# A fixed engine order over the sub-layer boundaries, paired adaLN units and a regrouped convolution in a two-layer hybrid trunk

## The chip, the cores and the metric

The kernel runs on one core of a Trainium2 chip. The metric is the device time of one execution in microseconds, taken as the median of several runs. The core's engines are PE (matrix products), PEld (the weight loads of PE), DVE (vector), ACT (scalar), POOL (GpSimd) and SP, whose queue issues the transfers.

## The reference

Two layers, each FFN, token mixer, FFN, are computed for two sets of 128 tokens of 1024 channels: the context tokens and the latent tokens. Both share the weights; they differ in the conditioning vector and in the start states of the scans.

```python
def _layer(x, cond, st, l, p, alpha):
    ada = (jax.nn.silu(cond) @ p['w_ada'][l] + p['b_ada'][l]).reshape(cond.shape[0], N_MOD, 1, D_MODEL)
    sh1, sc1, g1, sh2, sc2, g2, sh3, sc3, g3 = [ada[:, j] for j in range(N_MOD)]
    f1 = _swiglu(x * (1.0 + sc1) + sh1, p['ffn1_w_gate'][l], p['ffn1_w_up'][l], p['ffn1_w_down'][l])
    x = _layer_norm(alpha * x + 0.5 * g1 * f1, p['ln_g'][l, 0], p['ln_b'][l, 0])
    y, new_st = _mixer(x * (1.0 + sc2) + sh2, st, l, p)
    x = _layer_norm(alpha * x + g2 * y, p['ln_g'][l, 1], p['ln_b'][l, 1])
    f2 = _swiglu(x * (1.0 + sc3) + sh3, p['ffn2_w_gate'][l], p['ffn2_w_up'][l], p['ffn2_w_down'][l])
    x = _layer_norm(alpha * x + 0.5 * g3 * f2, p['ln_g'][l, 2], p['ln_b'][l, 2])
    return x, new_st
```

`_swiglu` is silu(h·w_gate)·(h·w_up) times w_down with 2816 hidden channels. `_mixer` multiplies h by `w_in`, runs a gated linear attention (GLA) and an mLSTM in both directions, the latter behind a three-tap convolution with silu, and merges both through `w_br_gla`, `w_br_mlstm` and `w_out`. The final states of the context tokens are outputs too. All is float32.

## The kernel before, in words

**Units.** A weight matrix is worked off in blocks of 512 columns, and a block in units of four k-tiles of 128 rows. A unit is two loads of 512 KB (`raw`, six buffers, issued on SP's queue). Each is split in two float32r parts, `hi` by ACT (L304) and `lo` by DVE (L305), seven buffers each, since a product is made of three: xh·hi (L320), xh·lo (L321), xl·hi (L322). A unit is twelve such matmuls for each of the two streams of tokens: stream 0 (context) works on unit i while stream 1 (latent) works on unit i−2 (`LAG`), so that each weight is split once and used twice.

**Sub-layers.** The six sub-layers (FFN, mixer, FFN, twice) are six phases of one list of units. Five boundaries lie between them. At one, each stream needs its last accumulator, then `ln_half` (L378 to L382: times the gate, plus the residual, statistics), `ln_finish` (L393 and L386 on DVE, the power on POOL at L387, the normalised `y` in two halves on DVE at L399), eight transposes on PE (L349), the modulation `mf` from PSUM by DVE and ACT in turn (L353, L355), and the split in `xh` (ACT L331) and `xl` (DVE L333). Only then can PE start the next phase for that stream. The residual x = y·g + b (L420, L421) follows on DVE a few units later.

**Order.** A scheduler orders each engine's instructions by priority, in the main by program order; `ln_half` and `ln_finish` of the boundaries stand in a higher priority (`PRIO`). The main loop at the program's end loads unit i+1, consumes unit i for stream 0 and unit i−2 for stream 1, and runs the due adaLN units.

**adaLN.** The shift, scale and gate vectors of later sub-layers are computed between the units: eight groups of two vectors each, a group of eight units (`ada_unit`), a unit of two 512 KB loads into `raw` buffers and four concurrent matmuls in the four column strips of PE (L168; the trace has eight records for them, since each takes two passes).

**Mixer.** `gates` (the input and forget gates of the mLSTM, with scans along time by DVE, L565 to L585) writes `Gd` to HBM (L589, SP's queue) and reads it back as `Db`, copied over the partitions (L598, SP's queue). DVE then masks `Db` (L610). The GLA follows heads by heads: `lal` (L333), `qk`, `E`, `kL` (L657 to L707, DVE), `att` (PE), `attT` (L722 to L725, DVE), `gla_o` (L728, PE). The convolution (L802 to L805) takes its middle tap on ACT and its outer taps on DVE.

## Time and profile before

| | us |
|---|---|
| runs | 1608.05, 1613.07, 1611.59 |
| median | 1611.59 |
| the profiled execution, its own time | 1617.74 |
| span of the profiled execution | 1615.9 |
| PE busy within the span | 1576.5 (98%) |
| DVE busy | 985.8 (61%) |
| ACT busy | 757.1 (47%) |
| POOL busy | 55.6 (3%) |

The span is what the trace covers; the profiled execution's own time is 1.84 us longer. The granted TensorE clock was 0.992 over the span. Busy PE includes time at a lower granted clock, so a stretch can look busy and still be slow. A wait is booked to the instruction that stood still and to what released it.

### The profile page before, as it was taken

The numbers are of one execution on the slowest core, as the hardware profiler recorded it, in microseconds if no ns is written. First come the engines' busy times: TensorE is split into PE (matmuls) and PEld (weight loads), VectorE is DVE, ScalarE is ACT, GpSimd is POOL, SyncE is SP. The second block draws the span as 40 slices with busy tenths as digits, with TensorE's granted clock in tenths as the row PEclk, the third lists the DMA queues.
The fourth block names the chain that finished last, engine by engine and source line by source line (L and its number), as shares of the span: only waits on it lengthen the run. The fifth ranks groups of instructions, "written<-read, shape, count | busy, mean of one in ns | idle before, by whom it ended". The sixth has DMA issues, their size and how long they took to land.

```text
span 1615.9 us, 20299 instructions
## 1 busy us (share of the span) xinstructions
PE 1576.5 (98%) x7323; PEld 1190.9 (74%) x7323; DVE 985.8 (61%) x1627; ACT 757.1 (47%) x1096; POOL 55.6 (3%) x102
## 2 busy tenths in 40 slices
PE   7999999999999999999999999999999999999997
PEld 3676677777777777777778878777777777777886
DVE  3544458666776568554566555775677665765555
ACT  2443334646556434444344444454755563444441
POOL 2000001000000000000000000100000000000000
PEclk9999999999999999999999999999999999999999
DMA  9777976666766776666865657665665767646661
GB/s 329 271 265 251 312 230 220 220 221 203 253 216 213 256 265 187 195 222 215 278 186 161 181 180 254 193 197 192 187 215 165 260 209 242 214 143 183 182 235 65
DMA packets 195981, 350.19 MB, mean 217 GB/s; under 512 B 17516, under 2 KB 73596, under 8 KB 195880
## 3 DMA queue, kind: packets, MB, share of 16 engines
q1 hardware_dynamic: 195320, 348.68, 66.7%
q8 instruction: 58, 0.95, 0.2%
q0 software_dynamic: 384, 0.13, 0.1%
q14 instruction: 43, 0.35, 0.1%
q10 hardware_dynamic: 176, 0.07, 0.0%
HBM read 341.30 MB, written 7.54 MB: 216 GB/s over the span
## 4 chain that ended last, share of the span: by engine, by line
PE 81%; issue 8%; DVE 5%; DMA 2%; ACT 2%; POOL 1%; SPq 0%; DVEq 0%; POOLq 0%; ACTq 0%
PE acc L320 23%; PE acc L322 22%; PE acc L321 22%; PE adaps L168 3%; DVE lo L305 2%; DMA araw<-in_w_ada 1%; PE hT L433 1%; PE num L837 1%; ACT hi L304 1%; PE num L834 1%; PE gps L531 1%; PE zps L630 0%; DMA Db<-Gd 0%; PE rg L814 0%; PE gla_o L728 0%
## 5 line engine op out<-in xcount | busy, mean ns | idle before, releaser
L305 DVE TENSOR_TENSOR lo<-raw,hi 128x1024 fp32r<-128x1024 f32 x456 | 557.0, 1223 | 355.6 <-ACT hi L304 347.3
L304 ACT ACTIVATE hi<-raw 128x1024 fp32r<-128x1024 f32 x456 | 481.6, 1059 | 413.5 <-PE acc L322 389.3
L320 PE MATMUL acc<-hi,xh 128*128 128x512 f32 x1280 | 516.5, 405 | 7.5 <-ACT xh L331 6.3
L321 PE MATMUL acc<-lo,xh 128*128 128x512 f32 x1280 | 513.1, 401 | 4.3 <-DVE lo L305 4.3
L322 PE MATMUL acc<-hi,xl 128*128 128x512 f32 x1280 | 514.1, 402 | 0.1
L320 PEld LDWEIGHTS acc<-hi,xh 128*128 128x128 f32 x1280 | 241.9, 189 | 105.0 <-issue 27.3
L321 PEld LDWEIGHTS acc<-lo,xh 128*128 128x128 f32 x1280 | 241.9, 189 | 60.4 <-DVE lo L305 9.0
L322 PEld LDWEIGHTS acc<-hi,xl 128*128 128x128 f32 x1280 | 242.3, 189 | 57.4 <-issue 4.2
L320 PE MATMUL acc<-hi,hid 128*128 128x512 f32 x320 | 126.8, 396 | 0.0
L321 PE MATMUL acc<-lo,hid 128*128 128x512 f32 x320 | 126.7, 396 | 0.0
L322 PE MATMUL acc<-hi,hid 128*128 128x512 f32 x320 | 126.4, 395 | 0.0
L168 PE MATMUL adaps<-araw,condp 128*32 128x512 f32 x512 | 74.2, 605 | 0.7 <-DMA araw<-in_w_ada 0.7
L320 PEld LDWEIGHTS acc<-hi,hid 128*128 128x128 f32 x320 | 60.1, 188 | 18.8 <-issue 4.2
L321 PEld LDWEIGHTS acc<-lo,hid 128*128 128x128 f32 x320 | 60.1, 188 | 14.4 <-issue 0.8
L322 PEld LDWEIGHTS acc<-hi,hid 128*128 128x128 f32 x320 | 60.1, 188 | 13.7
L331 ACT ACTIVATE hid<-hT 128x512 fp32r<-128x512 f32 x40 | 23.8, 597 | 82.5 <-PE hT L433 82.5
L321 PE MATMUL acc<-lo,oh 128*128 128x512 f32 x128 | 51.3, 401 | 0.0
L320 PE MATMUL acc<-hi,oh 128*128 128x512 f32 x128 | 51.1, 399 | 0.0
L322 PE MATMUL acc<-hi,ol 128*128 128x512 f32 x128 | 50.6, 395 | 0.0
L440 ACT ACTIVATE sg<-acc 128x512 f32<-128x512 f32 x40 | 23.8, 598 | 45.7 <-PE acc L322 45.7
L333 DVE TENSOR_TENSOR hid<-hT,hid 128x512 fp32r<-128x512 f32 x40 | 27.5, 691 | 28.0 <-ACT hid L331 28.0
L387 POOL TENSOR_TENSOR rstd<-rstd,mhalf 128x1 f32<-128x1 f32 x12 | 13.1, 1094 | 814.8 <-DVE rstd L386 800.7
(246 smaller groups left out, 1481.8 us busy)
## 6 DMA issues: line engine op xcount, KB each, us to landing
araw<-in_w_ada SPq DMA_DIRECT2D x128, 512.0 KB
raw<-in_w_in SPq DMA_DIRECT2D x96, 512.0 KB
raw<-in_ffn_w_down SPq DMA_DIRECT2D x88, 512.0 KB
raw<-in_ffn_w_gate SPq DMA_DIRECT2D x80, 512.0 KB
raw<-in_ffn_w_up SPq DMA_DIRECT2D x80, 512.0 KB
raw<-in_w_in SPq DMA_DIRECT2D x96, 256.0 KB
araw<-in_w_ada SPq DMA_DIRECT2D x32, 256.0 KB
raw<-in_w_br_gla SPq DMA_DIRECT2D x16, 512.0 KB
```

What stands on the lines that cost most here:

```text
L168: T.matmul(ps[32 * q:32 * q + 32, :], lhsT=condp[:, k, :], rhs=raw[q], start=(k == 0), stop=(k == KT - 1), tile_position=(0, 32 * q))
L304: A.activation(hi, raw, AF.Copy)
L305: V.tensor_tensor(lo, raw, hi.bitcast(F32), ALU.subtract)
L320: T.matmul(acc, lhsT=xh, rhs=wh, start=(k == 0), stop=False)
L321: T.matmul(acc, lhsT=xh, rhs=wl, start=False, stop=False)
L322: T.matmul(acc, lhsT=xl, rhs=wh, start=False, stop=(k == b.nk - 1))
L331: a = A.activation(dst_h, src, AF.Copy, scale=scale)
L333: v = V.tensor_tensor(dst_l, src, dst_h.bitcast(F32), ALU.subtract)
L433: T.transpose(pt[:, t, :], h[:, 128 * t:128 * (t + 1)], ident)
L440: A.activation(sg[s], acc, AF.Silu)
L531: T.matmul(ps[0:48, :], lhsT=wgt[:, k, :], rhs=mf[s][:, k, :], start=(k == 0), stop=(k == KT - 1))
L834: T.matmul(num, lhsT=sT[:, d, :], rhs=vh, start=True, stop=(s == 0))
```

## The change

Five boundaries get a function `boundary(e)`, which writes down the order of DVE, ACT and PE by hand, from the last unit e of a phase over the first three of the next. In it the first half of stream 1's down product (`half0`) is handed to DVE late, the normalised `y` is made half by ACT and half by DVE (which needs a small operation more, `nm`), `mf` is made four tiles by DVE and four by ACT, splits of the next units stand at given places, and two adaLN units fill a place in front of stream 1's transposes. The residual of both streams is made in one go two steps later. The raised priority is gone. In the FFNs the first unit of a down block takes the odd two k-tiles, where before the last one did.

adaLN units are spread anew over the phases. In the FFNs they come two at a time, eight matmuls in a row, and are loaded two units earlier into buffers of a general pool; in the mixers they come singly. None is broken up by other matmuls. Two groups have one vector only, which adds a copy, a matmul of 512 columns (`adaf`) and an addition each.

In the convolution ACT's four operations come first and DVE's eight behind them. In the mixer `gates` is called three units later, with the work behind it where it was, and the loads of ACT's function tables move to the boundaries.

```diff
+    ada_w = {}
+    def ada_load(grp, k, own):
+        raw = ada_w[grp, k] = []
+        for i in range(2):
+            l, v = grp[i % len(grp)]
+            kk = k if len(grp) == 2 else 2 * k + i
...
-        if k == 0:
-            ada_t[grp] = ms("adaps", [512])
-        ps = ada_t[grp]
-        for q in range(4):
-            T.matmul(ps[32 * q:32 * q + 32, :], lhsT=condp[:, k, :], rhs=raw[q],
-                     start=(k == 0), stop=(k == KT - 1), tile_position=(0, 32 * q))
-        if k < KT - 1:
-            return
+    def ada_units(todo):
+        with tc.manual_schedule(engines={T.engine}):
+            for grp, k in reversed(todo):
+                raw = ada_w.pop((grp, k))
+                i = ada_n[grp] = ada_n.get(grp, 0) + 1
+                if i == 1:
+                    ada_t[grp] = ms("adaps", [512])
+                for q in reversed(range(4)):
+                    kk = k if len(grp) == 2 else 2 * k + q // 2
+                    T.matmul(ada_t[grp][32 * q:32 * q + 32, :], lhsT=condp[:, kk, :], rhs=raw[q],
+                             start=(i == 1), stop=(i == parts(grp)), tile_position=(0, 32 * q))
+        for grp in dict.fromkeys(g for g, _ in todo):
+            if ada_n[grp] == parts(grp):
+                ada_sum(grp)
...
-        V.tensor_tensor(ar, ps, bt, ALU.add)
+        if len(grp) == 1:
+            V.tensor_copy(ar, ps)
+            ps = ms("adaf", [512])
+            T.matmul(ps[0:64, :], lhsT=fold2, rhs=ar, start=True, stop=True)
+            ar = t2("adar", [512])
+            V.tensor_tensor(ar[0:64, :], ps[0:64, :], bt[0:64, :], ALU.add)
+        else:
+            V.tensor_tensor(ar, ps, bt, ALU.add)
...
-            n = min(step, b.nk - k0)
+            n = (b.nk - k0) % step or step
...
+    def consume(s, u, j0=0, j1=None, defer=False):
...
+        if k0 > 0 and b.mid is not None:
+            b.mid(s)
...
-        for j in range(n):
+        for j in range(j0, n if j1 is None else j1):
...
-        if k0 + n == b.nk:
-            b.post(s, b.acc.pop(s))
+        done = k0 + n == b.nk and j1 is None
+        def post():
+            if done:
+                b.post(s, acc)
+        if done:
+            b.acc.pop(s)
+        if defer:
+            return post
+        post()
...
+    def modulate(s, xn, l, sub, between):
 
...
+        pts = []
         for g in range(2):
-            mod_tiles(s, xn, l, sub, range(4 * g, 4 * g + 4))
-
-    def mod_tiles(s, xn, l, sub, ks):
-        pt = ms("xT", [4, 128])
-        for j, k in enumerate(ks):
-            T.transpose(pt[:, j, :], xn[:, 128 * k:128 * (k + 1)], ident)
-        for j, k in enumerate(ks):
-            gm_, bm_ = modF[:, l, sub, s, 0, k:k + 1], modF[:, l, sub, s, 1, k:k + 1]
-            if j % 2 == 0:
-                V.tensor_scalar(mf[s][:, k, :], pt[:, j, :], gm_, bm_, ALU.mult, ALU.add)
-            else:
-                A.activation(mf[s][:, k, :], pt[:, j, :], AF.Identity, scale=gm_, bias=bm_)
-        sl = slice(ks[0], ks[-1] + 1)
-        g = int(ks[0] > 0 and len(ks) == 4)
-        fin["A", s, g], fin["V", s, g] = split_fm(xh[s][:, sl, :], xl[s][:, sl, :], mf[s][:, sl, :])
-
...
+            pt = ms("xT", [4, 128])
+            pts.append(pt)
+            for j in range(4):
+                k = 4 * g + j
+                T.transpose(pt[:, j, :], xn[:, 128 * k:128 * (k + 1)], ident)
+        def gb(k):
+            return modF[:, l, sub, s, 0, k:k + 1], modF[:, l, sub, s, 1, k:k + 1]
+        for k in range(4):
+            V.tensor_scalar(mf[s][:, k, :], pts[0][:, k, :], *gb(k), ALU.mult, ALU.add)
+        for k in range(4, 8):
+            if k == 6:
+                split_fm(xh[s][:, 0:4, :], xl[s][:, 0:4, :], mf[s][:, 0:4, :])
+                between()
+            gm_, bm_ = gb(k)
+            A.activation(mf[s][:, k, :], pts[1][:, k - 4, :], AF.Identity, scale=gm_, bias=bm_)
+        split_fm(xh[s][:, 4:8, :], xl[s][:, 4:8, :], mf[s][:, 4:8, :])
...
-            for n in range(2):
-                sl = slice(512 * n, 512 * n + 512)
-                V.tensor_scalar(y[:, sl], y[:, sl], mv[:, 0:1], r, ALU.subtract, ALU.mult)
-        if idx + 1 < n_sub:
             l2, sub2 = divmod(idx + 1, 3)
-            modulate(s, y, l2, sub2)
-            later.append([3, s, y, lnbc["g"], lnbc["b"], fin["V", s, 1]])
+            def apply():
+                nm = sm("nm", 1)
+                V.scalar_tensor_tensor(nm, mv[:, 0:1], -1.0, r, ALU.mult, ALU.mult)
+                A.activation(y[:, 512:], y[:, 512:], AF.Identity, scale=r, bias=nm)
+                V.tensor_scalar(y[:, :512], y[:, :512], mv[:, 0:1], r, ALU.subtract, ALU.mult)
+            def features(between):
+                modulate(s, y, l2, sub2, between)
+                later.append([s, y, lnbc["g"], lnbc["b"]])
+            steps[s] = apply, features
...
     def residuals():
 
-        for e in later:
-            e[0] -= 1
-        while later and later[0][0] <= 0:
-            _, s, y, g, b, behind = later.pop(0)
-            with tc.issue_after(behind):
+        while later:
+            s, y, g, b = later.pop(0)
+            with tc.issue_after(fin["lo"]):
...
-                for j in range(4):
-                    ch = 2 * h + j if j < 2 else 8 + 2 * h + j - 2
+                chs = [2 * h + j if j < 2 else 8 + 2 * h + j - 2 for j in range(4)]
+                for j, ch in enumerate(chs):
                     A.activation(yh[:, j, :], pt[:, j, :], AF.Identity, scale=conv_w(l, 1, ch), bias=conv_b(l, ch))
+                for j, ch in enumerate(chs):
...
+        units[first + 3][0].mid = gates
...
+            adas(((0, 8), (1, 2)), ((1, 0), (1, 1))),
+            adas(((1, 3), (1, 4)), ((1, 5),)),
...
+    def boundary(e):
+        u, u1, u2, u3 = units[e:e + 4]
+        fill = jobs[u1[4]][:2]
+        load(u1, 0)
+        load(u2, 0)
+        for a in fill:
+            ada_load(*a, True)
+        load(u3, 0)
+        with tc.manual_schedule(engines={V.engine, A.engine, T.engine}):
+            if u1[4] % 3 > 0:
+                tables = ("natural_log_exp_and_others", "silu_and_others")[u1[4] % 3 - 1]
+                tc.keep_in_program_order(A.preload_act_table_set(tables))
+            split_half(u1, 0)
+            consume(0, u)
+            half0 = consume(1, units[e - 2], defer=True)
+            split_half(u1, 2)
+            apply, features = steps.pop(0)
+            apply()
+            consume(1, units[e - 1])
+            features(lambda: split_half(u2, 0))
+            split_half(u2, 2)
+            half0()
+            consume(1, u)
+            split_half(u3, 0)
+            consume(0, u1)
+            consume(0, u2)
+            apply, features = steps.pop(1)
+            apply()
+            split_half(u3, 2)
+            ada_units(fill)
+            consume(0, u3, 0, 2)
+            features(lambda: None)
+            consume(0, u3, 2)
+    i = s0
+    while i < n + LAG:
+        if i + 1 < n and last(i):
+            boundary(i)
+            i += 3
+            continue
+        if i + 1 < n:
+            load(units[i + 1])
+        if i < n and not last(i - 3):
             consume(0, units[i])
         if i - LAG >= s0:
             consume(1, units[i - LAG])
-        if ahead and last(i - LAG):
-            with tc.issue_after(fin["V", 0, 0]), tc.issue_after(fin["A", 0, 0]):
-                load(ahead)
-        residuals()
+        if i - s0 > 2 and last(i - 5):
+            residuals()
         if i < n:
-            for a in due[i]:
-                ada_unit(*a)
+            for a in due_load[i]:
+                ada_load(*a, units[i][4] % 3 != 1)
+            ada_units(due[i])
+        i += 1
...
```

DVE at the second boundary (mixer to FFN in the first layer), around the normalisation of stream 1; `lo` is a weight split, `mv` the statistics, `mf` the modulated features, `x` the residual (`x_132` before and `x_133` now are stream 1's). Before:

```order
L378 TENSOR_TENSOR y<-acc_5459,gbc 128x512
L382 BN_STATS bst<-y 128x6
L381 SCALAR_TENSOR_TENSOR y<-x_132,y 128x512
L305 TENSOR_TENSOR lo<-raw,hi 128x1024
L382 BN_STATS bst<-y 128x6
L305 TENSOR_TENSOR lo<-raw,hi 128x1024
L393 BN_AGGR mv<-bst 128x2
L420 TENSOR_TENSOR x_131<-y,lngbc 128x1024
L386 TENSOR_SCALAR rstd<-mv 128x1
L305 TENSOR_TENSOR lo<-raw,hi 128x1024
L399 TENSOR_SCALAR y<-y,mv,rstd 128x512 x2
L421 TENSOR_TENSOR x_131<-x_131,lnbbc 128x1024
```

and now:

```order
L427 TENSOR_TENSOR y<-acc_5409,gbc 128x512
L430 SCALAR_TENSOR_TENSOR y<-x_133,y 128x512
L431 BN_STATS bst<-y 128x6
L427 TENSOR_TENSOR y<-acc_5492,gbc 128x512
L430 SCALAR_TENSOR_TENSOR y<-x_133,y 128x512
L431 BN_STATS bst<-y 128x6
L442 BN_AGGR mv<-bst 128x2
L435 TENSOR_SCALAR rstd<-mv 128x1
L334 TENSOR_TENSOR lo<-raw,hi 128x1024
L450 SCALAR_TENSOR_TENSOR nm<-mv,rstd 128x1
L452 TENSOR_SCALAR y<-y,mv,rstd 128x512
L334 TENSOR_TENSOR lo<-raw,hi 128x1024
```

The residual has left the stretch; both halves of stream 1 now stand in one row, a `lo` stands right behind `rstd` as it did, and DVE makes one half of `y`.

DVE in the first mixer, from the gates' last result `mc`, which is what `Gd` is written from, to the first `E` of the GLA. Before:

```order
L579 TENSOR_SCALAR mc<-pp_119,m0col_122 32x128 x4
L305 TENSOR_TENSOR lo<-raw,hi 128x1024
L585 TENSOR_TENSOR mt<-cumS,GT 128x8 x2
L305 TENSOR_TENSOR lo<-raw,hi 128x1024
L636 SCALAR_TENSOR_TENSOR ela<-zps,ela 128x512
L333 TENSOR_TENSOR lal<-ela,lah 128x512
L305 TENSOR_TENSOR lo<-raw,hi 128x1024
L657 COPY qk<-qkT 128x256
L701 TENSOR_TENSOR E<-E,qk 128x2x64
```

and now:

```order
L629 TENSOR_SCALAR mc<-pp_119,m0col_122 32x128 x4
L635 TENSOR_TENSOR mt<-cumS,GT 128x8 x2
L334 TENSOR_TENSOR lo<-raw,hi 128x1024 x2
L686 SCALAR_TENSOR_TENSOR ela<-zps,ela 128x512
L377 TENSOR_TENSOR lal<-ela,lah 128x512
L660 SCALAR_TENSOR_TENSOR Db<-Db,gpad,mk 128x128 x3
L334 TENSOR_TENSOR lo<-raw,hi 128x1024
L660 SCALAR_TENSOR_TENSOR Db<-Db,gpad,mk 128x128 x5
L707 COPY qk<-qkT 128x256
L751 TENSOR_TENSOR E<-E,qk 128x2x64
```

The eight masks of `Db` now stand between `lal` and `qk`; before, the first of them came 32 rows behind `mc`. The second mixer reads the same.

SP's queue at that place, before:

```order
L589 DMA Gd<-mc 128x128
L294 DMA raw<-in_w_in 128x2x512
L591 DMA out_m<-mt 1x4
L592 DMA out_m<-mt 1x4
L294 DMA raw<-in_w_in 128x2x512
L161 DMA araw<-in_w_ada 128x1024 x2
L294 DMA raw<-in_w_in 128x2x256 x8
L161 DMA araw<-in_w_ada 128x1024
L598 DMA Db<-Gd 128x512
```

and now:

```order
L639 DMA Gd<-mc 128x128
L641 DMA out_m<-mt 1x4
L642 DMA out_m<-mt 1x4
L323 DMA raw<-in_w_in 128x2x512
L648 DMA Db<-Gd 128x512 x2
```

Of thirteen weight loads between the write and the first read back, one is left.

## Rows read from the trace of the kernel before

**Rows 1.** The page's engine line: busy us (share), instructions.
```profile
PE 1576.5 (98%) x7323; PEld 1190.9 (74%) x7323; DVE 985.8 (61%) x1627; ACT 757.1 (47%) x1096; POOL 55.6 (3%) x102
```

**Rows 2.** The page's costliest group: count, busy us, mean ns, idle before and releaser.
```profile
L305 DVE TENSOR_TENSOR lo<-raw,hi 128x1024 fp32r<-128x1024 f32 x456 | 557.0, 1223 | 355.6 <-ACT hi L304 347.3
```

**Rows 3.** Waits of PE over the span: total us, times, longest.
```profile
PE acc L320 <- ACT xh L331: 6.3, 3, 2.3
...
PE acc L321 <- DVE lo L305: 4.3, 6, 1.0
PE xT L349 <- DVE y L399: 3.5, 7, 0.9
...
PE gla_o L728 <- DVE attT L725: 2.6, 2, 2.5
```

**Rows 4.** Windows: length, PE busy, PEld, DVE, ACT, POOL, granted clock, DMA share, GB/s.
```profile
645.00:655.00 10.00, 7.68 (x28) 5.82 (x27) 7.40 (x11) 4.88 (x9) 0.00 (x0) 0.83 0.15 48
839.00:850.00 11.00, 9.18 (x35) 6.76 (x35) 10.21 (x17) 5.82 (x10) 1.46 (x1) 0.84 0.48 144
1094.00:1105.00 11.00, 8.53 (x26) 6.62 (x26) 4.60 (x15) 4.25 (x9) 0.64 (x2) 0.69 0.53 170
1423.00:1435.00 12.00, 9.67 (x36) 7.41 (x35) 9.01 (x12) 5.83 (x9) 0.00 (x0) 0.86 0.27 83
```

**Rows 5.** Timeline of PE at boundaries 2 and 3: start, us, instruction, [idle before].
```profile
648.15 0.50 PE L320 MATMUL acc<-hi,xh 128*128 128x512 f32 x1 [2.32 <-ACT xh L331]
...
841.69 0.50 PE L320 MATMUL acc<-hi,xh 128*128 128x512 f32 x1 [1.61 <-ACT xh L331]
```

**Rows 6.** Timeline of PE, adaLN: a piece of a cut unit, two half units, a whole one.
```profile
64.08 1.04 PE L168 MATMUL adaps<-araw,condp 128*32 128x512 f32 x2
...
185.95 0.39 PE L321 MATMUL acc<-lo,xh 128*128 128x512 f32 x1
186.19 0.39 PE L322 MATMUL acc<-hi,xl 128*128 128x512 f32 x1
186.50 1.85 PE L168 MATMUL adaps<-araw,condp 128*32 128x512 f32 x8
...
1092.44 1.07 PE L168 MATMUL adaps<-araw,condp 128*32 128x512 f32 x8
```

**Rows 7.** Timeline of POOL and DVE: normalisation at boundaries 3 (first row) and 2.
```profile
837.25 0.55 POOL L387 TENSOR_TENSOR rstd<-rstd,mhalf 128x1 f32<-128x1 f32 x1 [115.84 <-DVE rstd L386]
...
641.68 1.22 DVE L305 TENSOR_TENSOR lo<-raw,hi 128x1024 fp32r<-128x1024 f32 x1
...
641.85 1.46 POOL L387 TENSOR_TENSOR rstd<-rstd,mhalf 128x1 f32<-128x1 f32 x1 [14.16 <-DMA araw<-in_w_ada]
...
643.34 1.00 DVE L399 TENSOR_SCALAR y<-y,mv,rstd 128x512 f32<-128x512 f32 x2 [0.44 <-POOL rstd L387]
```

**Rows 8.** Groups of DVE over the span: count, busy us, mean ns, idle before.
```profile
L382 DVE BATCH_NORM_STATS2 bst<-y 128x6 f32<-128x512 f32 x24 | 16.6, 691 | 0.4
...
L353 DVE TENSOR_SCALAR mf<-xT,modF 128x128 f32<-128x128 f32 x40 | 15.2, 407 | 2.0 <-PE xT L349 1.3 <-ACT mf L355 0.4
...
L420 DVE TENSOR_TENSOR x<-y,lngbc 128x1024 f32<-128x1024 f32 x10 | 12.1, 1210 | 0.0
...
L610 DVE SCALAR_TENSOR_TENSOR Db<-Db,gpad,mk 128x128 f32<-128x128 f32 x32 | 9.9, 350 | 6.5 <-DMA Db<-Gd 6.5
```

**Rows 9.** SP's queue (layer 1), chain of waits and PE (layer 2): the way of Db.
```profile
283.18 0.34 SPq L589 DMA_DIRECT2D Gd<-mc  x1
...
303.30 0.42 SPq L598 DMA_DIRECT2D Db<-Gd  x1
...
1087.34 7.76 DMA Db<-Gd
...
1096.65 0.79 PE L728 MATMUL gla_o<-vg,attT 128*128 128x256 f32 x1 [2.48 <-DVE attT L725]
```

**Rows 10.** Group of ACT in the convolution.
```profile
L802 ACT ACTIVATE yh<-mqkT,convF 128x128 f32<-128x128 f32 x64 | 28.9, 451 | 23.7 <-DVE yh L805 19.0 <-PE mqkT L798 4.6
```

More of the change, by code (lines that the diff above doesn't have):

```diff
@@ L30 @@
 SLOTS = 21
-PRIO = 100
 @with_exitstack
@@ L288, in load @@
             if part == 1:
-                raw = w.pop("raw")
-                split_w(raw, w, h)
+                split_w(w.pop(("raw", h)), w, h)
                 continue
@@ L296, in load @@
             if part == 0:
-                w["raw"] = raw
+                w["raw", h] = raw
             else:
@@ L304, in split_w, with split_half @@
         A.activation(hi, raw, AF.Copy)
-        V.tensor_tensor(lo, raw, hi.bitcast(F32), ALU.subtract)
+        fin["lo"] = V.tensor_tensor(lo, raw, hi.bitcast(F32), ALU.subtract).ins
         for j in range(2):
             w[h + j] = (hi[:, j, :], lo[:, j, :])
-    def consume(s, u):
+    def split_half(u, h):
+        w = u[3]
+        split_w(w.pop(("raw", h)), w, h)
+    def consume(s, u, j0=0, j1=None, defer=False):
         b, k0, n, w, _ = u
-        if k0 == 0:
+        if k0 > 0 and b.mid is not None:
+            b.mid(s)
+        if k0 == 0 and j0 == 0:
             if b.pre is not None:
@@ L469, in f @@
             def f(s, acc):
[L470 to L473 removed]
+                ln_half(s, n, acc, 0.5)
+                if n == 1:
+                    ln_finish(s, l, sub)
             return f
@@ L922, in mixer @@
             dict(v=b_v, k=b_k, n=b_n, q=b_q, r=b_r, g=b_gg, m=b_gm, o=b_o)[t[0]](int(t[1]))
-        b0 = units[first][0]
-        pre0 = b0.pre
-        def first_pre(s):
-            gates(s)
-            if pre0 is not None:
-                pre0(s)
-        b0.pre = first_pre
+        units[first + 3][0].mid = gates
         def bg_post(n):
@@ L966, in f @@
             def f(s, acc):
-                with tc.high_priority(offset=PRIO):
-                    ln_half(s, n, acc, 1.0)
-                    if n == 1:
-                        ln_finish(s, l, 1)
+                ln_half(s, n, acc, 1.0)
+                if n == 1:
+                    ln_finish(s, l, 1)
             return f
@@ L989, in adas @@
     def adas(*grps):
-        return [(g, k) for g in grps for k in range(KT)]
+        return [(g, k) for g in grps for k in range(parts(g))]
     jobs = [adas(((0, 2), (0, 5)), ((0, 3), (0, 4))),
-            adas(((0, 6), (0, 7)), ((0, 8), (1, 2)), ((1, 0), (1, 1))),
-            adas(((1, 3), (1, 4))),
-            [],
-            adas(((1, 5), (1, 8)), ((1, 6), (1, 7))),
-            []]
-    due = []
-    for p in range(6):
-        c, m = sum(u[4] == p for u in units), len(jobs[p])
-        first = 8 if p == 0 else 0
-        e = c - first - (6 if p % 3 != 1 else 8)
-        done = 0
-        for j in range(c):
-            upto = m * max(0, min(j + 1 - first, e)) // e
-            due.append(jobs[p][done:upto])
-            done = upto
+            adas(((0, 6), (0, 7))),
+            adas(((0, 8), (1, 2)), ((1, 0), (1, 1))),
+            adas(((1, 3), (1, 4)), ((1, 5),)),
+            adas(((1, 6), (1, 7))),
+            adas(((1, 8),))]
+    due_load, due = [], []
+    for p in range(6):
+        c = sum(u[4] == p for u in units)
+        step = 2 if p % 3 != 1 else 1
+        todo = jobs[p][0 if p == 0 else 2:]
+        first = 10 if p == 0 else 5
+        places = c - first - (7 if p % 3 != 1 else 10)
+        groups = [todo[a:a + step] for a in range(0, len(todo), step)]
+        at = [first + places * a // max(1, len(groups)) for a in range(len(groups))]
+        ld, mm = [[] for _ in range(c)], [[] for _ in range(c)]
+        for a, g in zip(at, groups):
+            ld[a - 2] += g
+            mm[a] += g
+        due_load += ld
+        due += mm
     for t in range(2):
@@ L1060, in last @@
         return 0 <= i < n and (i == n - 1 or units[i + 1][4] != units[i][4])
-    for i in range(s0, n + LAG):
-        ahead = units[i + 1] if i + 1 < n else None
-        if ahead and not last(i - LAG):
-            load(ahead)
-        if i < n:
+    def boundary(e):
[40 more added lines that the diff above has]
+        if i < n and not last(i - 3):
             consume(0, units[i])
```

30 lines of the change are left out of this document (14 added, 16 removed).

## The prediction

> **What bounds the kernel now.** I read the page's engine line first: PE is busy 1576.5 us of the span [rows 1]. So the kernel ends when PE's work ends, and a change can win only three things: work that PE no longer does, idle time of PE, and time in which PE runs at the lower granted clock. The waits of PE come next. Leaving the start of the program out they are few: 6.3 us in three waits for `xh`, 4.3 for `lo`, 3.5 for `y` in seven, 2.6 for `attT` [rows 3]. The waits for `xh` and for `y`, and about 1.4 of those for `lo`, lie at the five boundaries: 11.2 us. The longest stand in the timeline of PE, 2.32 us at boundary 2 and 1.61 at boundary 3 [rows 5]; boundary 5 repeats boundary 2. The third view is windows behind the long waits. PE's granted clock is 0.83 over 10 us behind boundary 2, 0.84 over 11 behind boundary 3, 0.86 over 12 behind boundary 5, and 0.69 over 11 in the second mixer behind the wait for `attT` [rows 4]: stretches at the lower of the two levels, 1.2 GHz of 2.4. They cost 0.17·10 = 1.7, 0.16·11 = 1.8, 0.14·12 = 1.7 and 0.31·11 = 3.4 us. The boundaries thus cost 11.2 + 5.2 = 16.4 us, the second mixer's wait 2.6 + 3.4 = 6.0. Behind the waits of up to 0.9 us that boundaries 1 and 4 have [rows 3] the clock stayed up.
>
> DVE is not the bound over the span, but at the boundaries it is the engine that is waited for: it has each `lo` of 1.22 us [rows 2] besides the normalisation.
>
> **adaLN: units no longer cut, and in pairs.** 64 units are to be done. A whole one takes PE 1.07 us [rows 6]. A piece of a cut unit takes nearly as long, 1.04 for two of the eight records [rows 6], since the four column strips run beside one another. In the trace five of the 64 are cut in two, so five pieces too many: 5 · 1.04 = 5.2 us, about 5.0 as the last passes overlap with what follows. One unit had its halves one behind the other, 1.85 us instead of 1.07 [rows 6]: 0.8 more. The changed program has 25 pairs and 14 single units, none cut: 5.8 us are saved. A pair is two groups of four strips in a row. The nearest row is just that unit of two half groups, 1.85 us, as the second group of strips starts before the first has ended; two single units take 2.14. That is 0.29 a pair, 25 · 0.29 = 7.2 us. From both sides: 0 if the second unit of a pair gains nothing, and 10 if the entry of a second unit behind other matmuls, which the row doesn't hold (186.19 to 186.50 is 0.31 where 185.95 to 186.19 is 0.24), goes too. I take 7.2. The two groups of one vector add a matmul of 512 float32 columns in two passes each; the nearest row is the piece of 1.04, so 2.0 for both (0 to 4 with a wait for the copy on DVE). Sum −5.8 − 7.2 + 2.0 = −11.0 us, bounds −16 and −2.
>
> **The boundaries.** I followed the new order by hand, from the end of stream 0's last unit. PE has 2·2.8 us of stream 1 (twelve matmuls of 0.24, [rows 6]), the transposes (about 1), stream 1's last unit, two units of stream 0 in the new phase, the pair of 1.85, half a unit, and stream 1's transposes: these begin at about 18.4. DVE in that time: stream 0's three operations per half of 0.69 [rows 8], then POOL's power, then `nm` and half of `y`: ready at 5.5, where PE is free at 5.6. The first stream is covered. Then four `mf` of 0.41 [rows 8], the two `xl` behind ACT, and two `lo` of 1.22 between them: DVE is free at about 13.3, although stream 1's sum lay ready at 9.9. Its three operations, `rstd` and POOL end at 17, `y` at 18. So the transposes don't wait, but the `lo` of the third unit that stands behind `y` comes 1.0 late, and `xh` 0.4 to 0.9: 1.6, 1.9 and 1.6 us of wait at boundaries 1, 3 and 4. At boundaries 2 and 5 the deferred half of stream 1 adds three operations, 2.1 us: the `lo` of the third unit's first half then comes 2.1 late, and with the others it is 4.0 each. Sum 13.1 us, where it was 11.2. The lower clock: it came behind 1.6 us and not behind 0.9; now the longest wait in one piece is 2.1, the others 1.0 or less. I count one stretch of 1.7. So 13.1 + 1.7 − 16.4 = −1.6 us. Bounds: all hidden, −16.4; and three stretches more with 4 us of wait, +9.
>
> POOL's power is in that chain. It took 0.55 us where DVE did nothing beside it, and 1.46 where a `lo` ran [rows 7]. In the new order a `lo` stands right behind `rstd` on DVE at every boundary, so I used 1.46 throughout. The Trainium skill, "SBUF — State Buffer", section "Who interferes with whom", says that a DVE instruction with two inputs in SBUF contends with a GpSimd instruction that reads SBUF, and that the second to issue blocks in full. The trace agrees: 1.46 is 0.55 plus most of a `lo`. The rule speaks against this order; without the contention the five chains would be 0.9 shorter each and the sum 4.5 us lower.
>
> **The residuals.** Four operations of 1.21 us [rows 8] now follow one another on DVE. DVE waits 347 us of the span for `hi` [rows 2], and the next pair gives it 1.85 us of PE's time; I count 0. If that cover is gone, 4.8 − 1.85 less the lead of half a unit, 1.4, is 1.6 a boundary, and 8 for five; 0 on the other side, as no row has PE waiting for a residual.
>
> **The mixer.** `gates` moves three units down, the GLA stays. DVE now reaches the masks of `Db` soon: behind `mc` there are `mt`, two `lo`, `ela` and `lal`, with their waits about 5 us. `Db` is then not there. Its read took 7.76 us in the chain of waits [rows 9], and it can be issued only when `Gd` has been written. No row shows that write's landing; it lies between 0 and the 7.76 of the read. It moves a small part of the read's bytes, so I take 2.5. `Db` is ready at 10.3, DVE stands for 5, and `qk`, `E`, `kL` and every `lo` stand behind it. Eight masks of 0.35 [rows 8], a `lo` and the steps to `kL` take 5.5 more, so `att` can start at 15.8, where PE reaches it at about 13.3 by its order. I count 2.5 us of wait and 1.7 of the lower clock, in each mixer: 8.4, where 6.0 are paid now. That is +2.4 us. Bounds: −6.0 if the masks wait for nothing, +13 if the write is as slow as the read. SP's queue is no obstacle by itself: between write and read it has one `raw` load, where the read was issued 20.1 us behind the write before [rows 9].
>
> **The convolution.** ACT waited 19.0 us for DVE's steps there [rows 10], but PE's waits [rows 3] name no operation of it. I take −0.5, between 0 and −1.5. Moving the table loads and the odd k-tiles of the down blocks I count at nothing: the same instructions, beside PE's matmuls.
>
> **Sum.** −11.0 − 1.6 + 2.4 − 0.5 = −10.7 us. The working is from the profiled execution of 1617.74 us, which becomes 1607.0. The runs' median lies 6.2 lower, at 1611.59, and becomes 1600.9: I forecast 1601.
>
> **Rivals.** (A) *`Db` holds DVE for long.* If the write lands as late as the read (7.76 instead of 2.5) and the `raw` load ahead of the read on SP's queue waits for a buffer for one unit of one stream (2.8), each mixer waits 8.1 us longer and gets a second stretch of 1.7: +19.6, 1621, slower than before. It turns the result from about 4 us later per mixer on. For it: the masks stand directly behind `lal`. Against it: the same read cost DVE 6.5 us in all before [rows 8]. Chance 0.13. (B) *The boundaries are hidden in full*, which would be so if DVE's splits had more lead than I give them: 16.4 instead of 1.6, 1586. Against it stands the power at 1.46. Chance 0.15. (C) *The pairs come late.* Four 512 KB loads now follow one another on SP's queue ahead of weights; if weights or the pair's own data land late, PE waits or the 7.2 us are lost: 1609. For it: before, adaLN loads were spread singly. Chance 0.12. (D) *The change doesn't do what it says at the boundaries*: the waits only move to stream 1 and grow, and the residuals are not covered, +6 to +9: 1608. Chance 0.10. The forecast has 0.50.
>
> **Chances and range.** A measurement of this kernel can tell about 0.3%, 4.8 us, from no change. Faster by more (below 1606.8): 0.47 of the forecast, B, and 0.08 of C and D, 0.70. Slower by more (above 1616.4): 0.10, from A. Between: 0.20. The range 1587 to 1612 leaves out half of B below and most of A above, and takes in C, D and the forecast's bounds of −6 for the mixers and 0 for the pairs.
>
> **What would show it.** In the changed profile: adaLN pairs of about 1.85 us on PE, and none cut; PE's waits at boundaries 1 to 5 of 1.6, 4.0, 1.9, 1.6, 4.0, for `lo` and `xh`, none for `y` of stream 0; rows of `rstd` on POOL at 1.46; DVE standing some 5 us for `Db` in each mixer, and PE for `attT`, `att` or `lo` behind it, 2.5. The prediction is wrong if pairs take 2.1, if PE's waits for weights' `lo` or for the loads rise by over 5 us in the first FFN, or if the granted clock is low in a place that has no wait now.

## The result and the profile after

The changed kernel takes 1592.32 us (median of four runs, 1591.93 to 1592.54), the kernel before 1612.30 beside it: a ratio of 0.9881, 95% interval 0.9863 to 0.9899. It is 20.0 us faster, where 10.7 were forecast. The sign and the range held; the gain was nearly twice the forecast. The profiled execution took 1591.93 us, 0.4 below the median, and its span is 1590.1. The profiled execution of before, 1617.74, was 5.4 us above the median beside it, so of the 25.8 us between the two spans some 5 belong to that one execution.

The page's engine line, as [rows 1]:

```profile
PE 1556.1 (98%) x7327; PEld 1188.5 (75%) x7327; DVE 985.0 (62%) x1631; ACT 762.2 (48%) x1106; POOL 58.1 (4%) x103
```

DVE does the same work. PE is busy 20 us less, with four instructions more. Where that went shows in four views. The waits of PE (total, times, longest), as [rows 3]:

```profile
PE acc L356 <- DVE lo L334: 8.4, 12, 1.3
...
PE cfin L913 <- DVE nf L915: 2.8, 8, 0.4
...
PE acc L355 <- ACT xh L375: 0.9, 3, 0.3
```

The waits for `xh` fell from 6.3 us to 0.9. Those for `y` (3.5) and for `attT` (2.6) have no row any more. Those for `lo` rose to 8.4, of which 5.5 lie at the boundaries. The timeline of PE at boundary 2, as [rows 5]:

```profile
610.23 1.92 PE L183 MATMUL adaps<-araw,condp 128*32 128x512 f32 x16
...
613.87 0.50 PE L356 MATMUL acc<-lo,xh 128*128 128x512 f32 x1 [1.29 <-DVE lo L334]
...
617.53 0.50 PE L356 MATMUL acc<-lo,xh 128*128 128x512 f32 x1 [0.77 <-DVE lo L334]
...
619.47 0.50 PE L355 MATMUL acc<-hi,xh 128*128 128x512 f32 x1 [0.28 <-ACT xh L375]
```

Three waits of 2.3 us in all stand where 4.0 were forecast, and in the forecast order: a `lo` of the third unit, its other `lo`, then `xh`. In the same way boundary 5 has 2.3, boundary 3 0.85, boundaries 1 and 4 0.45: 6.4 us, where 13.1 were forecast and 11.2 stood before. Windows behind the same places as [rows 4] (columns as there):

```profile
613.00:623.00 10.00, 8.00 (x35) 5.88 (x36) 6.54 (x12) 6.42 (x10) 1.70 (x2) 1.00 0.52 158
826.00:837.00 11.00, 10.15 (x47) 7.54 (x46) 8.07 (x11) 5.85 (x10) 0.00 (x0) 1.00 0.55 164
1094.00:1105.00 11.00, 11.00 (x62) 8.18 (x61) 8.08 (x21) 8.53 (x15) 0.00 (x0) 1.00 0.77 219
1391.00:1403.00 12.00, 10.09 (x44) 7.34 (x45) 8.33 (x13) 7.48 (x11) 1.61 (x2) 1.00 0.45 131
```

The granted clock is 1.00 in all four. In this execution it is low at the start and the end of the program only. That is 8.6 us won against [rows 4].

adaLN, the pairs in the timeline of PE and its group (busy us, mean ns, idle before):

```profile
105.59 1.92 PE L183 MATMUL adaps<-araw,condp 128*32 128x512 f32 x16
107.44 0.50 PE L355 MATMUL acc<-hi,xh 128*128 128x512 f32 x1
107.78 0.40 PE L356 MATMUL acc<-lo,xh 128*128 128x512 f32 x1
108.02 0.40 PE L357 MATMUL acc<-hi,xl 128*128 128x512 f32 x1
...
L183 PE MATMUL adaps<-araw,condp 128*32 128x512 f32 x512 | 63.0, 600 | 0.1
```

A pair holds PE 1.85 us (105.59 to 107.44), and none is cut. The matmul behind it takes 0.34 us to the next, where 0.24 is usual; the step into a piece is some 0.09 longer than usual too. From its start to the start of the matmul behind it, all pieces came to 69.5 us before (69 pieces) and 60.3 now (39): −9.2. Thirty pieces fewer, at 0.09 and 0.10 us for the steps in and out, are an estimated 5.7 more: −14.9.

The mixer: SP's queue, and DVE's masks.

```profile
313.77 0.34 SPq L639 DMA_DIRECT2D Gd<-mc  x1
...
316.12 0.89 SPq L648 DMA_DIRECT2D Db<-Gd  x2
...
319.86 0.69 DVE L377 TENSOR_TENSOR lal<-ela,lah 128x512 fp32r<-128x512 f32 x1 [0.70 <-ACT lah L375]
321.41 0.88 DVE L660 SCALAR_TENSOR_TENSOR Db<-Db,gpad,mk 128x128 f32<-128x128 f32 x3 [0.85 <-DMA Db<-Gd]
```

The read is issued 2.35 us behind the write (20.1 in [rows 9]) and has landed 5.3 us later. DVE waits 0.85 us for it in the first mixer and not at all in the second. PE waits neither for `att`'s inputs nor for `attT`.

Between the two profiles the sum is: adaLN −14.9 with +2.2 for the two added matmuls; waits at the boundaries −4.8; lower clock there −5.2; the second mixer's wait and clock −5.9; a wait of 1.0 for `lo` in the first mixer gone; and some 2 us of small waits more (`cfin` 2.8 where it was 1.6, and others). That is −27.6, 1.8 more than the −25.8 between the spans; 0.3 of the lower clock lies inside the wait for `attT`, where it costs nothing, and for the rest it isn't settled which term is too large.

### The profile page after: what moved, and what is told of

Its sections match the earlier page's. It is cut to its first block, busy times and chain, and to the rows that moved or that the text cites. A ratio compares the mean times of both kernels' runs of the same rounds, so it can differ in the third digit from the quotient of the medians.

```text
span 1590.1 us, 20320 instructions
## 1 busy us (share of the span) xinstructions
PE 1556.1 (98%) x7327; PEld 1188.5 (75%) x7327; DVE 985.0 (62%) x1631; ACT 762.2 (48%) x1106; POOL 58.1 (4%) x103
## 4 chain that ended last, share of the span: by engine, by line
PE 82%; issue 7%; DVE 5%; ACT 2%; DMA 2%; POOL 1%; SPq 0%; DVEq 0%; POOLq 0%; ACTq 0%
PE acc L355 23%; PE acc L356 23%; PE acc L357 23%; PE adaps L183 3%; DMA araw<-in_w_ada 2%; DVE lo L334 2%; PE hT L486 1%; ACT hi L333 1%; POOL rstd L436 1%; PE num L888 1%; PE num L885 1%; PE gps L583 1%; PE oT L822 0%; PE sfin L793 0%; PE gla_o L778 0%
## 5 line engine op out<-in xcount | busy, mean ns | idle before, releaser
L183 PE MATMUL adaps<-araw,condp 128*32 128x512 f32 x512 | 63.0, 600 | 0.1
L377 DVE TENSOR_TENSOR hid<-hT,hid 128x512 fp32r<-128x512 f32 x40 | 27.6, 692 | 33.4 <-ACT hid L375 33.4
L436 POOL TENSOR_TENSOR rstd<-rstd,mhalf 128x1 f32<-128x1 f32 x12 | 16.6, 1387 | 740.1 <-DVE rstd L435 740.1
```

The lines of the kernel that those rows point to most:

```text
L183: T.matmul(ada_t[grp][32 * q:32 * q + 32, :], lhsT=condp[:, kk, :], rhs=raw[q], start=(i == 1), stop=(i == parts(grp)), tile_position=(0, ...
L377: v = V.tensor_tensor(dst_l, src, dst_h.bitcast(F32), ALU.subtract)
L436: G.tensor_tensor(r, r, mhalf[:, 0:1], ALU.pow)
```

## The experiments

Twelve kernels ran, in three groups of four; each time is a median of four to ten runs beside runs of before on the same chip. The first group undoes one part of the change each, the second takes the boundary apart, the third puts parts into the kernel before and looks for a faster one. The changed kernel itself came out at 1591.86 in the second group, and every difference to it below is taken from that figure. The kernel before came out at 1610.04, 1610.62 and 1611.23 in the three groups, so differences of about 1 us across groups say nothing.

**The boundaries ordered as before.**

```diff
-    def boundary(e):
+    fill = {}
+    for i in range(s0, n + LAG):
...
+            fill[i + 3] = jobs[ahead[4]][:2]
...
+        if i in fill:
+            ada_units(fill[i])
```

> The changed kernel, but with the boundaries ordered as before: raised priority, alternating mf, both halves of y on DVE, no fixed order; pairs, convolution and gates as changed. Theory 1 (idle and clock): the new order is worth the 4.8 us less of idle time of PE at the five boundaries and the 5.2 us of lower clock behind them, so this kernel is some 10 us slower than the changed one, about 1602 us, with the waits for xh of 1.6 to 2.3 us back and a stretch of granted clock 0.5 behind boundaries 2, 3 and 5. Theory 2 (the forecast's term was right): the boundaries are worth 1.6 us, so about 1594, and the rest of the gain lies in the adaLN part.

Measured 1601.59 us, ratio to before 0.9944 (0.9926 to 0.9962): 9.7 us slower than the changed kernel. The size is that of theory 1, but its mechanism is not there. The timeline of PE at boundary 2 and windows behind boundaries 2 and 5:

```profile
621.55 1.08 PE L394 MATMUL xT<-ident,y 128*128 128x128 f32 x8 [0.52 <-DVE y L446]
622.56 1.92 PE L184 MATMUL adaps<-araw,condp 128*32 128x512 f32 x16
...
625.66 0.50 PE L356 MATMUL acc<-hi,xh 128*128 128x512 f32 x1 [0.29 <-ACT xh L376]
...
620.00:632.00 12.00, 10.90 (x56) 7.14 (x57) 9.92 (x15) 5.85 (x9) 1.12 (x2) 1.00 0.32 89
...
1402.00:1415.00 13.00, 11.76 (x60) 7.52 (x59) 10.92 (x15) 5.83 (x9) 1.63 (x2) 1.00 0.32 91
```

In [rows 5] PE waited 2.32 us for `xh` at this place. Here the pair of adaLN units stands in that wait, 0.29 is left, and the clock stays up. So the old order doesn't bring the long waits back as long as the pair is there. What it costs are many small ones: `y` 4.5 us, `xl` 2.1, and 2.1 for `E` in the mixers, where ACT loads a table just ahead of `E` (1.28 us) and no longer at the boundary. Where they cost time can be read from the starts of stream 0's transposes at the five boundaries. They lie 0.4, 5.1, 4.3, 5.1 and 9.6 us behind those of the changed kernel as it ran in the second group, and the end of PE's work 9.7. So 4.6 and 4.4 us are lost from boundary 1 to 2 and from 4 to 5, that is on the way into and through the two mixers, and 0.3 in all from boundaries 2, 3 and 5 on through the FFNs behind them: with the pair there, the old order is as good as the new one at these three. The edit also moves the table loads back, so how much of the 9 us in the mixers is theirs isn't separated.

**Units one at a time in the FFNs.**

```diff
-        step = 2 if p % 3 != 1 else 1
+        step = 1
```

> The changed kernel with the FFNs' adaLN units one at a time (unbroken, still loaded two units ahead); the pairs inside the five boundaries stay. Theory 1: a pair takes 1.95 us of PE and two single units 2.17, so 20 pairs give back 4.5 us: about 1597. Theory 2 (pairs are worth more, through fewer breaks of the matmul stream or through the loads): 8 us or more, 1600 or above.

Measured 1598.31 us (0.9925, 0.9908 to 0.9943), 6.5 slower. Theory 1 has the place, at 0.32 us a pair instead of 0.22: the pieces came to 63.0 us against 60.3, and there are 20 more of them with their steps in and out, 0.19 us each as above: 2.7 + 3.8.

**The convolution as before.**

```diff
-                for j, ch in enumerate(chs):
+                for j in range(4):
                     A.activation(yh[:, j, :], pt[:, j, :], AF.Identity, scale=conv_w(l, 1, ch), bias=conv_b(l, ch))
-                for j, ch in enumerate(chs):
```

> The changed kernel with the convolution's ACT and DVE operations interleaved as before. Theory 1: off PE's path, 0 to 0.5 us slower, 1592 to 1593. Theory 2: PE's products in the mixer wait for yh, 2 us or more slower.

Measured 1599.96 us (0.9936, 0.9919 to 0.9954): 8.1 slower, theory 2. PE's waits show where, in the mLSTM's last products (`cfin`) and behind the gating of the mixer's outputs (`th`):

```profile
PE cfin L912 <- ACT kw L905: 3.9, 4, 1.0
PE cfin L912 <- DVE nf L914: 3.5, 8, 0.6
...
PE acc L355 <- DVE th L816: 1.6, 4, 0.4
```

Both mixers take 4 us longer, of which 3 are waits that one can see.

**The gates at the mixer's first unit.**

```diff
-        units[first + 3][0].mid = gates
...
+        b0.pre = first_pre
```

> The changed kernel with the gates back at the mixer's first unit. Theory 1: the wait for Db that held DVE, attT and PE for 2.5 us in the second mixer of the kernel before, and the 3.4 us of lower clock behind it, came from the gates' early place with the read issued 20 us behind the write; they return in one or both mixers: 1596 to 1602. Theory 2: what delayed the read was the adaLN loads on SP's queue, which are fewer now in the mixers; then this kernel is within 1 us of the changed one. The forecast's rival (Db holds DVE longer in the changed order) would have this kernel faster by 2 us or more.

Measured 1612.77 us (1.0018, 1.0009 to 1.0028), 20.9 slower. None of the theories expected that much. The waits of PE, and DVE's and PE's timelines in the first mixer:

```profile
PE gpT L588 <- DVE ag L586: 13.4, 2, 6.9
...
PE acc L355 <- ACT hi L333: 5.2, 3, 2.1
...
309.48 0.88 DVE L660 SCALAR_TENSOR_TENSOR Db<-Db,gpad,mk 128x128 f32<-128x128 f32 x3 [3.48 <-DMA Db<-Gd]
...
315.26 0.73 PE L355 MATMUL acc<-hi,xh 128*128 128x512 f32 x2 [2.12 <-ACT hi L333]
```

The first unit lies inside the fixed order of the boundary. There DVE comes to the gates' copies only behind stream 1's sums, and PE, whose order is fixed too, stands 6.5 and 6.9 us for them, and the clock falls at each. So the move of the gates is no edit of its own: the fixed order as it is written needs it, as their new place is the first unit behind it. `Db` is heard of too, as theory 1 has it: its read is again issued 21 us behind the write, DVE stands 3.5 us for it in each mixer, ACT's operation on `Db` and the `hi` behind it come late, and PE waits 2.1 us for that `hi`, twice. The clock didn't fall there. That is 4.2 us of PE's waits; the two long ones weigh far more.

**The pair taken out of the boundary.**

```diff
-        fill = jobs[u1[4]][:2]
+        fill = []
...
-            ada_units(fill)
```

> The changed kernel without the adaLN pair inside the boundaries; the ten units are done in the FFNs and mixers like the others (23 pairs and 18 singles where it was 25 and 14, 0.4 us more of PE). Theory 1: the pair is what covers stream 1's way through DVE at the boundaries, so PE waits 1.95 us longer at boundaries 2 and 5, 1 to 1.9 us longer at the others, some 8 us in all, and behind waits above about 2 us the granted clock falls again, 1.7 us each at boundaries 2 and 5 or more: 1602 to 1606. Theory 2: the fixed order alone keeps PE fed, and the pair only stands where any other place would do: within 2 us of the changed kernel.

The measure beside it was the changed kernel once more:

> The changed kernel itself, as the measure for the kernels beside it on this chip: 1592 us, and the granted clock at 1.0 from 60 us to the last 10 us of the span.

The changed kernel: 1591.86 us (0.9880, 0.9865 to 0.9894). Without the pair: 1615.24 us (1.0025, 1.0015 to 1.0035), 23.4 slower, and slower than before. Theory 1 has the mechanism at the boundaries, and half of the loss lies elsewhere. Waits of PE, timeline at boundary 2, windows around its four long waits, and PE around `attT` in the first mixer, here and last in the changed kernel's first profile:

```profile
PE acc L356 <- DVE lo L334: 13.9, 11, 3.3
...
PE gla_o L778 <- DVE attT L775: 5.0, 2, 2.5
...
624.23 0.80 PE L356 MATMUL acc<-lo,xh 128*128 128x512 f32 x1 [3.26 <-DVE lo L334]
...
385.00:400.00 15.00, 11.99 (x46) 9.72 (x47) 11.48 (x34) 8.08 (x14) 0.66 (x1) 0.77 0.16 40
620.00:632.00 12.00, 8.63 (x34) 6.39 (x33) 8.98 (x16) 5.81 (x10) 1.48 (x1) 0.86 0.52 161
1176.00:1190.00 14.00, 11.08 (x48) 9.03 (x49) 11.70 (x34) 7.99 (x13) 0.66 (x1) 0.88 0.20 48
1408.00:1422.00 14.00, 10.70 (x39) 8.49 (x38) 10.62 (x20) 6.07 (x10) 1.48 (x1) 0.76 0.56 168
...
386.51 0.39 PE L770 MATMUL att<-E,EC 128*128 128x128 f32 x2
389.40 1.19 PE L778 MATMUL gla_o<-vg,attT 128*128 128x256 f32 x2 [2.50 <-DVE attT L775]
...
378.17 0.39 PE L770 MATMUL att<-E,EC 128*128 128x128 f32 x2
...
381.41 0.59 PE L778 MATMUL gla_o<-vg,attT 128*128 128x256 f32 x2
```

The waits at the boundaries are 5.4 us more (11.8 against 6.4). The clock falls at all four long waits, two at the boundaries and two in the mixers. By the windows this costs 3.5, 1.7, 1.7 and 3.4 us; in the first and the last the stretch begins inside the wait, so PE's work loses 3.0 and 2.8. A wait for `attT` stands in both mixers, where there are two more adaLN units each. It isn't the one of [rows 3]: that stood in stream 0, where a mask between the steps of `attT` waited for the read of `Db`. This one stands in stream 1, and no mask there waits for a read. The masks between the steps aren't its cause either, as the changed kernel has them at the same place and doesn't wait: it has thirteen matmuls of a weight unit between `att` and `gla_o`, and here there is none. Why PE has no unit left isn't followed further. Together the boundaries account for some 10 us (5.4 + 1.7 + 3.4) and the mixers for some 12 (5.0 and 2.0 of waits, 3.5 + 1.7). So this run shows the worth of the pair at the boundary together with that of fewer units in the mixers, about half and half.

**The split of the third unit ahead of stream 1's sums.**

```diff
+            split_half(u3, 0)
             half0()
             consume(1, u)
-            split_half(u3, 0)
```

> The changed kernel with the weight split of the third unit's first half on DVE and ACT ahead of stream 1's sums, not behind its rstd. Theory 1 (contention of DVE and POOL, and a late lo): POOL's power takes 0.55 us instead of 1.48, PE's wait of 1.3 us for that lo at boundaries 2 and 5 goes, and y of stream 1 comes no later, since the 1.2 us lost ahead of it are won back at the power: 3 to 4 us faster, 1588 to 1589. Theory 2 (DVE's queue is the bound, whatever its order): what is won at the power is lost ahead of it, within 1 us of the changed kernel.

Measured 1593.14 us (0.9890, 0.9875 to 0.9905), 1.3 slower: theory 2, if for 0.3 us beyond what it allowed. POOL's power did fall from 1.48 to 0.55 us, and the wait for `lo` went, but PE now waits as long for `y`, which comes later by the `lo` ahead of it:

```profile
613.25 0.55 POOL L436 TENSOR_TENSOR rstd<-rstd,mhalf 128x1 f32<-128x1 f32 x1 [13.77 <-DVE rstd L435]
...
614.70 1.06 PE L394 MATMUL xT<-ident,y 128*128 128x128 f32 x8 [1.57 <-DVE y L452]
617.10 0.50 PE L356 MATMUL acc<-lo,xh 128*128 128x512 f32 x1 [0.76 <-DVE lo L334]
...
1393.37 1.06 PE L394 MATMUL xT<-ident,y 128*128 128x128 f32 x8 [1.56 <-DVE y L452]
1395.78 0.60 PE L356 MATMUL acc<-lo,xh 128*128 128x512 f32 x1 [0.76 <-DVE lo L334]
...
612.00:624.00 12.00, 9.30 (x41) 6.54 (x40) 8.03 (x16) 7.59 (x11) 1.02 (x2) 1.00 0.33 94
1391.00:1403.00 12.00, 9.60 (x37) 7.17 (x36) 7.22 (x14) 7.01 (x11) 1.02 (x2) 0.86 0.32 93
```

The two boundaries have the same waits to 0.01 us, and the clock fell behind one and not behind the other. Waits of 1.6 us are where it is open.

**Stream 1's first half at once.**

```diff
-            half0 = consume(1, units[e - 2], defer=True)
+            consume(1, units[e - 2])
...
-            half0()
```

> The changed kernel with stream 1's first half normalised at once at boundaries 2 and 5, instead of behind stream 0's features. Theory 1: the 2.1 us on DVE then lie in stream 0's way, partly beside POOL's power; PE waits about 1 us for y of stream 0 and no longer 1.3 us for lo: within 1 us of the changed kernel, 1592. Theory 2 (the deferral is what costs the 4 us that were forecast at these two boundaries): 3 us faster, 1589.

Measured 1590.04 us (0.9868, 0.9854 to 0.9883), 1.8 faster, between the theories. At boundaries 2 and 5 PE waits 1.4 us for stream 0's `y`; the 1.3 us for `lo` are gone, and 0.6 is left of the 0.8:

```profile
601.50 1.06 PE L394 MATMUL xT<-ident,y 128*128 128x128 f32 x8 [1.44 <-DVE y L452]
...
616.05 0.50 PE L356 MATMUL acc<-lo,xh 128*128 128x512 f32 x1 [0.59 <-DVE lo L334]
```

**The new convolution in the kernel before.**

```diff
+                for j, ch in enumerate(chs):
                     A.activation(yh[:, j, :], pt[:, j, :], AF.Identity, scale=conv_w(l, 1, ch), bias=conv_b(l, ch))
+                for j, ch in enumerate(chs):
```

> The kernel before with the new order of the convolution alone (ACT's four operations first). Theory 1: the convolution is in PE's way only where the gates come three units later, as in the changed kernel, where its old order cost 8 us; here it is worth 0 to 1 us, 1610. Theory 2: it is worth its 8 us in any kernel: 1603.

Measured 1610.70 us (0.9998, 0.9987 to 1.0009): nothing, so theory 2 is out. ACT's wait for DVE (19.0 us, [rows 10]) costs nothing in that kernel. Theory 1 puts this down to the place of the gates. That is not shown: the first mixer of the kernel before also has 24 adaLN units between its own products where the changed one has 6 (and 2 at the boundary), and these two differences weren't tried apart.

**adaLN units at the boundaries of the kernel before.**

```diff
-            adas(((0, 6), (0, 7)), ((0, 8), (1, 2)), ((1, 0), (1, 1))),
-            adas(((1, 3), (1, 4))),
-            [],
+            adas(((0, 6), (0, 7))),
+            adas(((0, 8), (1, 2)), ((1, 0), (1, 1))),
+            adas(((1, 3), (1, 4))),
...
+            due.append((fill if j == 2 else []) + todo[done:upto])
```

> The kernel before with the adaLN groups spread so that two units stand due with the third unit of each phase behind boundaries 1 to 4 (boundary 5 can have none as long as groups are of two vectors); order, convolution and gates as before. Theory 1 (adaLN work at the boundary covers stream 1's way): the waits of 2.3 and 1.6 us for xh at boundaries 2 and 3 and the granted clock's fall behind them go, those at boundary 5 stay: 6 to 8 us faster than before, 1603. Theory 2 (it needs the fixed order): under 2 us faster, 1609 to 1611.

Measured 1606.40 us (0.9967, 0.9955 to 0.9979), 4.8 faster:

```profile
627.37 1.92 PE L168 MATMUL adaps<-araw,condp 128*32 128x512 f32 x16
...
630.48 0.50 PE L320 MATMUL acc<-hi,xh 128*128 128x512 f32 x1 [0.29 <-ACT xh L331]
...
829.97 0.50 PE L320 MATMUL acc<-hi,xh 128*128 128x512 f32 x1 [1.61 <-ACT xh L331]
...
841.43 1.92 PE L168 MATMUL adaps<-araw,condp 128*32 128x512 f32 x16
```

At boundary 2 the wait for `xh` fell from 2.3 to 0.3 us; at boundary 3 the scheduler set the units 11 us behind the wait of 1.6 us, which stayed, as did the 2.3 at boundary 5. So theory 1 holds where the units land in the wait, which needs an order that puts them there. For boundary 5 they don't exist without the groups of one vector. The edit also takes sixteen units out of the first mixer, and in its profile the second mixer's wait for `attT` (2.5 us in [rows 3]) is gone, and one of 1.4 stands in the first; so the 4.8 us aren't the boundaries' alone.

**Towards a faster version.** The first adds two edits to the run without deferral, the second puts more adaLN units ahead of stream 0's transposes.

```diff
             consume(0, u2)
+            hi_half(u3, 2)
             apply, features = steps.pop(1)
             apply()
-            split_half(u3, 2)
+            lo_half(u3, 2)
```

> The changed kernel with stream 1's first half normalised at once, ACT's part of the split of the third unit's second half ahead of y (the last wait of PE for lo behind the boundary, 0.3 to 0.8 us, was DVE waiting 1.3 us for that hi), and the small constant for the one-vector groups made after the start. Theory 1: on top of the 1.8 us of the first edit the waits of 0.6 and 0.3 us at each boundary go: 1587. Theory 2: ACT's y then comes later by what hi takes, and PE waits for y: 1590 to 1592.

```diff
+        return {2: 4, 5: 3}.get(p, 2)
...
+            ada_units(fill[2:])
             features(lambda: split_half(u2, 0))
```

> The kernel of the run before this, and at boundaries 2 and 5 two and one more adaLN units ahead of stream 0's transposes, where PE waited 1.4 us for y. Theory 1: the wait goes at no cost, as these units have to be done anyway: 2 to 3 us faster than the run before this, 1584. Theory 2: the loads of the added units come late or take buffers: no faster.

Measured 1589.59 us (0.9866, 0.9848 to 0.9884) and 1587.78 us (0.9855, 0.9838 to 0.9871). The first won 0.5 us where 3 were expected, which is no more than the groups differ by: the waits for `lo` and `xh` at the boundaries are gone, those of 1.4 us for stream 0's `y` stand, and in the first mixer a wait of 1.1 us for `lal` came up. The second won 1.8 where 2 to 3 were expected. It is 23.5 us faster than before and 4.1 faster than the changed kernel. Its waits of PE at the boundaries come to 0.3 us, so about nothing is left to win there:

```profile
PE acc L371 <- DVE lo L334: 2.9, 5, 0.8
PE cfin L928 <- DVE nf L930: 2.8, 8, 0.4
PE argA L738 <- DVE lal L392: 1.7, 2, 0.9
```

## Why the prediction was right, and where its size was off

**adaLN, −11.0 forecast: held.** −14.9 + 2.2 = −12.7 between the profiles. The five cuts were what they were taken for; an added matmul held PE 1.0 us. The price of a pair was right, for a reason that is half another: two groups in a row hold PE 1.85 us where two single units hold 2.00, so 0.15 come from the overlap, and about 0.19 from one step into and out of adaLN fewer, which the forecast had left to its bounds. Undoing 20 of the 25 pairs gave back 6.5 us where the pair term has 5.8 for 20.

**The boundaries, −1.6 forecast, −10.0 between the profiles: mis-sized.** The chain was right in its order: `lo`, `lo`, `xh`, with `y` of stream 0 covered, POOL's power at 1.48, and boundaries 2 and 5 worse than the others by the deferred half. They were taken some 1.3 us a boundary too long: 13.1 us where 6.4 were measured. Of the two parts of the sum here, the waits were most in error, by 6.7 us. Some 0.6 of the 1.3 is DVE's chain: it was free for stream 1's sums 7.1 us behind the start of stream 0's transposes (608.05 and 600.91 at boundary 2), where the forecast had 7.7 (13.3 and 5.6). For the rest no single step is named here. The clock adds 1.7: I counted one stretch left, and there was none. The run without the pair shows that it was near: waits of 3.3 us there, and low clock behind them. The forecast had the pair in its chain as one of PE's jobs, but it didn't ask which part of the gain was the pair's and which the order's. The run with the old order shows the long waits gone with the pair alone, the run without the pair shows long waits back in the new order. The order by itself, with the table loads, is worth 9.7 us, nearly all of it around the mixers, and it puts the pair in its place.

**The mixer, +2.4 forecast, about −7 between the profiles (−5.9 and −1.0): wrong in sign.** The steps that failed are DVE standing 5 us for `Db` and PE 2.5 us behind it, in each mixer: DVE stood 0.85 us in the first and not in the second, and PE not at all. DVE does come to the masks of `Db` as early in its queue as forecast. But it took 6.8 us from the write's issue to get there and not 5, since a `lo`, `lal` and `mt` waited (1.74, 0.70 and 0.48 us), and the read had landed 5.3 us behind its issue and not 7.8. Why it was faster isn't shown: in the run with early gates a read took 5.7 us with the DMA engines 87% busy, where the 7.8 had 91%. The 2.5 us taken for the write were long enough (2.35 to the read's issue). 2.35 + 5.3 − 6.8 is the stall of 0.85. So the sum put 8.4 in the place of the 6.0 that were paid before, and neither is paid now.

**The convolution, −0.5 forecast: a term that isn't one.** Alone it is worth nothing; in the changed kernel, with the gates three units later and fewer adaLN units in the mixers, it is worth 8.1; which of the two makes it count is open. A sum over parts can't show that: undone one by one, the parts cost 9.7, 6.5, 8.1, 20.9 and 23.4 us, three times the gain in all. The change is one piece.

**The residuals, 0 forecast:** no wait of PE of 0.25 us or more stands behind them in the FFNs of the changed kernel.

**The rivals.** (A), `Db` holding DVE, did not come; its condition, a slow write, wasn't met. (B), the boundaries hidden in full, is closest to what happened, though 6.4 us of waits were left: its 1586 is 6 us below the result, and the last version, where they are hidden, has 1587.8. Its chance of 0.15 looks too low. (C) and (D) did not come: PE's group of adaLN waits 0.1 us for its loads.

**Luck.** Three terms of the sum came out lower than forecast, by some 2, 8 and 9 us between the profiles. That the result still lay inside 1587 to 1612 is owed to the lower end of the range, which rival (B) had set, and not to the forecast's own account of the boundaries and mixers.

**What stays open.** Of the 25.8 us between the profiles the runs confirm 20; the kernel before had a mean granted clock of 0.992 in its profiled execution and 0.993 to 0.997 in others, where one stretch of 3.4 us at the lower level is 0.001. Why the clock falls behind 1.6 us of waiting in one place and not in another isn't settled. How the 23.4 us without the pair divide between the boundaries and the mixers, about half and half, is read from that profile only; it wasn't tried apart.

## What to carry to other kernels

When an engine has to wait for a chain at a known place, keep independent work of that engine for it, and check in the timeline that it lands there; here two units, 1.9 us together, were worth some 10 us at five boundaries. Before pricing a change of several parts as a sum, ask of each part whether it pays alone and what it makes necessary: the fixed order moved the gates, something in the new mixers made the convolution's order count, and the last boundary needed groups of one vector to have work at all. Here a wait that was followed by a stretch of lower clock cost its own length plus 1.7 to 3.1 us.

## What was unexpected of the hardware

The length of a wait alone doesn't tell whether the granted clock falls. Over all profiles of this study, outside the program's start, it fell at seven of seven waits of 2.5 us or more, at three of seven of 2.1 to 2.4 us, and at four of five of 1.6 us, three of them at boundary 3 of kernels with the old order; behind 1.29 and 0.77 us in a row it stayed at 1.00. DVE's `lo` beside POOL's power costs 0.93 us (1.48 against 0.55), as the Trainium skill, "SBUF — State Buffer", section "Who interferes with whom", has it for a DVE instruction of two SBUF inputs beside a GpSimd instruction that reads SBUF. The run with the early split shows that it can be undone without any gain, since the same `lo` then stands in the chain itself.
